# Differential attention with routed experts on one Trainium2 core: q/k/v projections five token tiles ahead of the scores instead of four

## The chip, the cores and the metric

The kernel runs on one core of one Trainium2 chip. The metric is the device time of one execution in microseconds (us). The engines named below are TensorE (PE; its weight loads are shown apart as PEld), VectorE (DVE), ScalarE (ACT), GpSimd (POOL) and SyncE (SP), which only issues DMAs. Each engine takes its instructions in the order in which it was given them.

## The reference, cut to what matters

One layer: RMS norm, differential attention, residual, RMS norm, a mixture of experts, residual. 1024 tokens, 1024 channels, 8 heads, two 64-wide halves of q and k in each head, float32 throughout.

```python
q, k, v = jnp.split(x @ w_in, [2 * H * dh, 4 * H * dh], axis=-1)
q = rmsnorm(q.reshape(B, T, H, 2, dh), q_gain) * (dh ** -0.5)
k = rmsnorm(k.reshape(B, T, H, 2, dh), k_gain)
sc = jnp.einsum('bqhcd,bkhcd->bhcqk', q[:, s:e], k[:, :e])
sc = jnp.where(dist >= 0, sc - slopes * dist, -jnp.inf)
p = jax.nn.softmax(sc, axis=-1)
pd = p[:, :, 0] - lam * p[:, :, 1]
o = rmsnorm(einsum('bhqk,bkhe->bqhe', pd, v[:, :e]), subln) * (1 - lambda_init)
x = x + o.reshape(B, T, H * 2 * dh) @ w_out
x = x + hier_moe(rmsnorm(x, norm_ffn))   # 16 experts, two for each token
```

## The kernel before

The tokens are cut into 8 tiles of 128 and the work of the attention into 64 steps, one for each pair of head h and tile t, numbered g = 8h + t. One loop (L765) runs over g; what it calls in one turn is issued in that order to each engine, and no scheduler moves it (`tc.manual_schedule()`, L37). Turn g does for its own tile the scores (`scores`, two matmuls per key block, high and low part), the bias and the row maximum on DVE (`biased`), the exponentials on ACT (`expo`) and the difference of the two softmaxes on DVE (`combine`). For the tile before, g - 1, it transposes the probabilities on PE (`pd_transpose`) and multiplies them with v (`pv`). The cost of scores, softmax and transposes grows with t, since a tile sees only the keys up to itself.

The same turn projects a tile that lies LEAD tiles ahead, q = g + LEAD: `qkv`, 24 matmuls of 384 columns in two parts of 12, each with the weight split in a high and a low part. At its end ACT and DVE take q, k and v out of PSUM and leave the sums of squares (ssq, L326). After every second tile `qk_norm` normalises the pair on POOL: 14 small instructions for the inverse root, then two products into the tile qn (L340). At odd g, `qk_transpose` (called from `crossings`, L351 and L353) transposes the pair that holds tile g + 1 on PE; ACT and DVE make the high and low parts KM, AH and AL from it. qn has one buffer, qk and ssq have two, vHL and vb thirteen.

The weights of the next heads are loaded by SP (`load_w`, at t == 3) and split into a high and a low part in 8 chunks (`split_w`: ACT makes wH, L243, DVE makes wL, L244), spread over the turns: one chunk in most turns, two at t = 3, none at t = 4.

When a head is done, `o_norm` normalises its output on POOL: 17 small instructions and two products (L458 to L464). For heads 0 to 5 this is issued at the end of the turn t = 1 of the next head, for head 6 already at t = 0 of head 7; `o_transpose` (L472) puts the result through PE at t = 4, for head 6 in the middle of the turn t = 2. For head 7 each tile has its own `o_norm1` on POOL (L522 to L528, 18 instructions), issued at the end of the turn after its scores, and its own `o_transpose1` on PE (L534).

As soon as no projections are left, g >= E0 = 64 - LEAD, the turns take up the output projection of tile e = g - E0 (`out_proj`, 48 matmuls), the residual (`residual`: store, square on ACT, inverse root on POOL) and the routing of the tiles before (`route_x`, `logits`, `route_r`, `route_i`). Before: e = 0 at g = 60, and the loop ends after g = 64 with e = 4. `late(5)` and `late(6)` do the two tiles after that without any attention in them, and `last` does tile 7. In `late(5)` o_transpose1(6) stands behind a third of an output projection; o_transpose1(7) follows after `late(5)`. Then the memory of the attention is given free (`es_att.close()`), and `moe_round` issues the loads of the first five weight tiles of the experts (1 MB each, L986, and three more as buffers come free) on SP before `late(6)`, which is called from `first_index`. Their first use is `split_h(0)` on ACT (L994), in the middle of `last`.

At the end of `last`, the rows of the tokens have been written to DRAM (xn_dram), and POOL gathers them by expert (L1011, L1017); the expert products begin with the gathered rows.

Of the kernel before, what the change touches and what calls it, by code (L numbers as in the profile page):

```python
# [7 lines left out]
F32 = mybir.dt.float32  # L8
F32R = mybir.dt.float32r
BF = mybir.dt.bfloat16  # L10
# [23 lines left out]
def trunk_layer_kernel(ctx, tc, a, out):  # L34
# [200 lines left out]
    def split_w(h, c):  # L235

        j = c // 3
        if c % 3 == 0:
            W["H", h, j] = w_tile([128, 3, 384], F32R, "wH")
            W["L", h, j] = w_tile([128, 3, 384], F32R, "wL")  # L240
        wh, wl, r = W["H", h, j][:, c % 3], W["L", h, j][:, c % 3], W["r", h, j][:, c % 3]
        g = gm[:, c:c + 1]
        act.activation(wh, r, AF.Copy, scale=g)  # L243
        vec.scalar_tensor_tensor(wl, r, g, f(wh), op0=OP.mult, op1=OP.subtract)  # L244
# [49 lines left out]
            other = slice(64 * (1 - c), 64 * (2 - c))  # L294
            vec.tensor_scalar(al[other, c], ident[other, None, :].to_broadcast([64, 2, 128]), 0.0, None, op0=OP.mult)
    QK, SS = {}, {}
    LEAD = 4

    def qkv(h, t, part):
        if part == 0:  # L300
            if h == 0 and t < LEAD and t % 2:
                qkv.ps = psQ.tile([128, 384], F32, name="qkv", tag="po", bufs=1)
            elif (8 * h + t >= LEAD and (t - LEAD) % NT in (0, 2)):
                qkv.ps = psS.tile([128, 384], F32, name="qkv", tag="sc")
            else:
                qkv.ps = psQ.tile([128, 384], F32, name="qkv", tag="qkv", bufs=1)
        ps = qkv.ps
        for c in range(4 * part, 4 * part + 4):
            for x, w in ((0, "H"), (0, "L"), (1, "H")):
                pe.matmul(ps, lhsT=hT[t][:, x, c], rhs=W[w, h, c // 3][:, c % 3],  # L310
                          start=(c == 0 and x == 0 and w == "H"), stop=(c == 7 and x == 1))
        if part == 1:
            rs = RX[t]
            if t % 2 == 0:
                QK[h, t // 2] = att.tile([128, 2, 4, 64], F32, name="qk", bufs=2)
                SS[h, t // 2] = att.tile([128, 2, 4], F32, name="ssq", bufs=2)
            qk = QK[h, t // 2][:, t % 2]
            act.activation(qk.rearrange("p a b -> p (a b)"), ps[:, :256], AF.Copy, scale=rs)
            v = att.tile([128, 2, 128], F32R, name="vHL", bufs=13)
            vb = att.tile([128, 128], BF, name="vb", bufs=13)  # L320
            VV[h, t] = v, vb
            act.activation(v[:, 0], ps[:, 256:], AF.Copy, scale=rs)
            vec.scalar_tensor_tensor(v[:, 1], ps[:, 256:], rs, f(v[:, 0]), op0=OP.mult, op1=OP.subtract)  # L323
            sq = att.tile([128, 4, 64], F32, name="sqk")
            act.activation(sq.rearrange("p a b -> p (a b)"), qk.rearrange("p a b -> p (a b)"), AF.Square)
            vec.tensor_reduce(SS[h, t // 2][:, t % 2], sq, axis=AX.X, op=OP.add)  # L326
            act.activation(vb, f(v[:, 0]), AF.Copy)
# [173 lines left out]
    def load_o(t):  # L501
        ORAW[t] = att.tile([128, H - 2, 128], F32, name="oraw")
        sp.dma_start(ORAW[t], o_view[:, :H - 2, t * 128:(t + 1) * 128])
# [243 lines left out]

    E0, LATE = NT * H - LEAD, 5  # L750
    def more_tokens(q):
        if q + 2 < NT:
            transpose_x(q + 2)
# [10 lines left out]

    for g in range(-LEAD, E0 + LATE):  # L765
        h, t = divmod(g, NT)
        q = g + LEAD
        e = g - E0
        if t == 0 and 0 <= h < H:
            vec.tensor_scalar(bias, bias, 0.5, None, op0=OP.mult)  # L770
        on(scores, g)
        on(biased, g, 0)
        if g > 2:
            crossings(g, h, t)
        on(expo, g, 0)
        on(biased, g, 1)
        if e >= 0:
            on1(out_proj, e, 0)
        on(qkv, q, 0)
        if t == 2 and h == H - 1:  # L780
            o_transpose(h - 1)
        on(pd_transpose, g - 1)
        on(expo, g, 1)
        on(combine, g)
        if 0 <= h < H - 1:
            if h == 0:
                chunks = {0: (0, 1), 1: (2,), 2: (3, 4), 3: (5, 6, 7)}.get(t, ())
            else:
                chunks = {0: (3,), 1: (4,), 2: (5,), 3: (6, 7)}.get(t, ())
            for c in chunks:  # L790
                split_w(h + 1, c)
        if t >= 5 and 0 <= h < H - 2:
            split_w(h + 2, t - 5)
        if 0 < e + NT < NT - 1:
            c = e + NT - 1
            split_wout(c)
            if c + 4 < NK:
                load_wout(c + 4)
        if e == -1:
            prep_o(0)  # L800
        if e >= 0:
            on1(route_x, e - 1)
            on1(route_i, e - 3)
            on1(route_r, e - 2)
            on1(prep_o, e + 1)
            on1(load_o, e + 2)
            on1(load_res, e + 1)
            on1(out_proj, e, 1)
            on1(o_transpose1, e + 1)
            route(e - 1)  # L810
            on1(residual, e)
        if q == 0:
            transpose_x(1)
            norm_x((2, 3), pool)
        if g <= 2:
            crossings(g, h, t)
        on(qkv, q, 1)
        on(pv, g - 1)
        if q == 0:
            more_tokens(q)  # L820
        if q % 2 and q < NT * H:
            qk_norm(q // NT, q % NT // 2)
        if t == (1 if h < H - 1 else 0) and 0 < h < H:
            o_norm(h - 1)
        if q > 0:
            more_tokens(q)
        if g == -LEAD:
            load_params()
        if g == -LEAD + 1:
            lambda_and_gains()  # L830
            load_w(1)
        if e == -2:
            load_o(0)
        if g == 9:
            routing_constants()
        if t == 3 and 0 <= h < H - 2:
            load_w(h + 2)
        if g == E0 - NT - 1:
            load_gain()
            for c in range(4):  # L840
                load_wout(c)
        if e == -1:
            for c in (NK - 2, NK - 1):
                split_wout(c)
            o_transpose1(0)
            load_o(1)
            load_res(0)
        on1(o_norm1, g - 1 - NT * (H - 1))
    def late(e):

        out_proj(e, 0, 0, 4)
        route_x(e - 1)
        route_i(e - 3, None, "tp")
        route_r(e - 2)
        flush()
        if e == LATE:
            prep_o(e + 1)
            o_transpose1(e + 1)
            load_o(e + 2)
        if e + 1 < NT:  # L860
            load_res(e + 1)
        out_proj(e, 0, 4, NK)
        route(e - 1)
        out_proj(e, 1)
        residual(e)
# [77 lines left out]
        return other_experts  # L943

    late(LATE)
    prep_o(LATE + 2)
    o_transpose1(LATE + 2)
    es_att.close()


# [344 lines left out]
            start(part)  # L1295

    def first_index(start):
        for e in range(LATE + 1, NT - 1):
            late(e)
        return last(start)  # L1300

    moe_round(first_index)
# [26 lines left out]
```

## Time and profile before

| | |
|---|---|
| time, three runs | 1018.61, 1018.22, 1013.28 us; median 1018.22 |
| the profiled execution's own time | 1017.58 us |
| its span, first to last instruction | 1015.7 us |
| busy: PE, DVE, ACT, POOL | 941.3, 816.4, 746.0, 338.1 us |
| granted TensorE clock, mean | 0.983 of full speed |
| attention, output projection and routing | 0 to about 637 us |
| experts | about 637 to 1000 us |

The busy time of PE comes from modelled ends of pipelined matmuls, so it is read here by what is missing: the gaps in which PE waits, what ended them, and the stretch of the kernel in which they lie. A row of the timeline gives start, duration, engine, line, operation, output and inputs, and in brackets the idle time of the engine just before it and what ended it.

### The profile page before, as it was taken

What the parts mean: (1) busy time and instruction counts of PE and PEld (TensorE: products, weight loads), DVE (VectorE), ACT (ScalarE), POOL (GpSimd) and SP (SyncE); (2) the same over time, 40 slices, a digit from 0 to 9 for tenths busy, and PEclk for the clock granted to TensorE, in tenths of its full rate; (3) what the DMA queues carried; (4) which work ended last, traced back from release to release, by engine and by line L of the source; (5) the groups of instructions that cost most, each with busy time, mean ns of one, the idle gap of its engine ahead of it and who ended that gap; (6) DMA issues with size and microseconds to landing.
All of it is one profiled execution on the core that took longest, in us unless ns stands there. A gap on an engine that the chain in (4) does not pass through costs nothing. (4 is left out here: it accounts for less than half of the span.)

```text
span 1015.7 us, 20013 instructions
## 1 busy us (share of the span) xinstructions
PE 941.3 (93%) x7241; PEld 875.5 (86%) x7241; DVE 816.4 (80%) x1719; ACT 746.0 (73%) x1577; POOL 338.1 (33%) x1009
## 2 busy tenths in 40 slices
PE   8989999999999999998999998799999999999992
PEld 8889899998989999888788886689989999999982
DVE  5788787887888787887768769799888899889880
ACT  7777777777777777777643325489899989898971
POOL 4523624425252442517764622201122212122011
PEclk9999999999999999999999999899999999999997
DMA  6220200202011020311323376789999999999923
GB/s 213 84 66 1 64 22 1 84 2 84 1 50 35 2 84 1 125 44 57 111 87 110 127 291 248 263 298 321 344 340 339 341 352 332 339 324 337 339 55 52
DMA packets 75770, 161.72 MB, mean 159 GB/s; under 512 B 8712, under 2 KB 39440, under 8 KB 67472
## 3 DMA queue, kind: packets, MB, share of 16 engines
q1 hardware_dynamic: 70544, 141.87, 39.4%
q0 software_dynamic: 5120, 18.50, 7.9%
q8 instruction: 59, 0.97, 0.4%
q14 instruction: 47, 0.39, 0.1%
HBM read 139.05 MB, written 21.30 MB: 158 GB/s over the span
## 5 line engine op out<-in xcount | busy, mean ns | idle before, releaser
L310 PE MATMUL qkv<-wH,hT 128*128 128x384 f32 x1024 | 291.3, 346 | 8.1 <-DVE vHL L323 6.9
L1003 DVE TENSOR_TENSOR mL<-raw,mH 128x2048 bf16<-128x2048 f32 x95 | 215.7, 2284 | 5.7 <-ACT mH L994 5.6
L310 PEld LDWEIGHTS qkv<-wH,hT 128*128 128x128 f32 x1024 | 188.2, 189 | 12.1 <-DVE vHL L323 10.4
L994 ACT ACTIVATE mH<-raw 128x2048 fp32r<-128x2048 f32 x95 | 177.8, 1902 | 1.2 <-POOL rs_x L56 1.2
L310 PE MATMUL qkv<-wL,hT 128*128 128x384 f32 x512 | 172.2, 336 | 0.4 <-DVE wL L244 0.4
L1069 PE MATMUL gu<-xT,mH 128*128 128x280 f32 x1024 | 153.4, 299 | 2.4 <-DVE gt L1099 1.3
L1069 PEld LDWEIGHTS gu<-xT,mH 128*128 128x128 f32 x1024 | 136.4, 190 | 3.2 <-DVE gt L1099 1.8
L1203 POOL DMA_INDIRECT out_dram<-yo,sidx x20 | 33.7, 1687 | 282.3 <-ACT yo L1201 251.6
L404 ACT ACTIVATE st<-st,nm 128x256 f32<-128x256 f32 (+7 forms) x128 | 99.2, 775 | 15.8 <-DVE nm L400 14.5
L1074 PEld LDWEIGHTS <-mL 128*128 128x128 bf16 x1536 | 94.0, 97 | 6.2
L310 PEld LDWEIGHTS qkv<-wL,hT 128*128 128x128 f32 x512 | 97.1, 190 | 0.7 <-DVE wL L244 0.7
L400 DVE CUSTOM_DVE_ANT_0 st<-sc,bias 128x256 f32<-128x256 f32 (+7 forms) x128 | 93.6, 750 | 2.3 <-PE sc L392 0.2
L1069 PE MATMUL gu<-hx,mH 128*128 128x280 f32 x512 | 82.0, 302 | 6.8 <-DVE yT L1099 6.2
L449 ACT ACTIVATE sqo<-ou 128x128 f32<-128x128 f32 x64 | 19.9, 311 | 92.3 <-DVE ou L447 92.3
L425 DVE TENSOR_TENSOR pdL<-tp,pdH 128x512 bf16<-128x512 f32 (+2 forms) x96 | 50.6, 554 | 45.0 <-ACT pdH L424 45.0
L550 PE MATMUL op<-wo,oH 128*128 128x512 f32 x256 | 82.2, 403 | 0.3 <-DVE xres L553 0.3
L334 POOL TENSOR_SCALAR ssq<-ssq 128x8 f32<-128x8 f32 x32 | 6.3, 198 | 226.8 <-DVE ssq L326 226.6
L1069 PEld LDWEIGHTS gu<-hx,mH 128*128 128x128 f32 x512 | 68.8, 189 | 9.2 <-DVE yT L1099 8.2
L1074 PE MATMUL gu<-xb,mL 128*128 128x140 bf16 x1024 | 74.3, 224 | 0.0
L391 PE MATMUL sc<-KM,AH 128*128 128x384 f32 (+4 forms) x192 | 65.5, 347 | 0.0
L392 PE MATMUL sc<-KM,AL 128*128 128x384 f32 (+4 forms) x192 | 65.0, 344 | 0.0
L411 DVE SCALAR_TENSOR_TENSOR st<-st,sm,st 128x128 f32<-128x128 f32 (+3 forms) x64 | 62.8, 981 | 2.3
(238 smaller groups left out, 1996.8 us busy)
## 6 DMA issues: line engine op xcount, KB each, us to landing
raw<-in_moe_w_gate_dram SPq DMA_DIRECT2D x32, 1024.0 KB, 7.4
raw<-in_moe_w_up_dram SPq DMA_DIRECT2D x32, 1024.0 KB, 6.2
raw<-in_moe_w_down_dram SPq DMA_DIRECT2D x31, 1024.0 KB, 8.1
wraw<-in_da_w_in_dram SPq DMA_DIRECT2D x64, 192.0 KB, 3.1
out_dram<-xres SPq DMA_DIRECT2D x9, 512.0 KB
xraw<-in_x_dram SPq DMA_DIRECT2D x8, 512.0 KB, 5.5
woraw<-in_da_w_out_dram SPq DMA_DIRECT2D x8, 512.0 KB, 5.2
xres<-in_x_dram SPq DMA_DIRECT2D x8, 512.0 KB, 4.3
```

Source lines behind the costliest of these rows:

```text
L310: pe.matmul(ps, lhsT=hT[t][:, x, c], rhs=W[w, h, c // 3][:, c % 3], start=(c == 0 and x == 0 and w == "H"), stop=(c == 7 and x == 1))
L391: pe.matmul(ps[:, k, :wc], lhsT=AH[h, t][:, c], rhs=KM[h][:, c, ks], start=True, stop=False)
L392: pe.matmul(ps[:, k, :wc], lhsT=AL[h, t][:, c], rhs=KM[h][:, c, ks], start=False, stop=True)
L400: vec.tensor_tensor_reduce(sv, tiles[c][:, :n, :wc], bv, -1.0, 3e38, OP.add, OP.min, nm[:, c:c + 1])
L404: act.activation(st[c][:, :w], st[c][:, :w], AF.Exp, scale=-1.0, bias=nm[:, c:c + 1], accum_out=sm[:, c:c + 1])
L411: vec.scalar_tensor_tensor(st[0][:, :w], st[1][:, :w], sm[:, 3:4], st[0][:, :w], op0=OP.mult, op1=OP.add)
L425: vec.tensor_sub(pl[:, g:g + n], ps[:, :n], f(ph[:, g:g + n]))
L550: pe.matmul(ps, lhsT=o[:, c], rhs=wo[4 * half + c // 2][:, w, c % 2], start=(c == 0 and o is oh and w == 0), stop=(c == NK - 1 and o is ol))
L994: act.activation(WH[g], full[g], AF.Copy)
L1003: vec.tensor_sub(WL[g], full[g], f(WH[g]))
L1069: pe.matmul(res[i // 2][:, i % 2, :2 * CAP], lhsT=wh[:, c - c0, 128 * i:128 * i + 128], rhs=rhs[:, c].rearrange("p a b -> p (a b)"), start ...
L1074: pe.matmul(res[i // 2][:, i % 2, :CAP], lhsT=wl[:, c - c0, 128 * i:128 * i + 128], rhs=rb[:, c], start=False, stop=stop, skip_group_check ...
```

## The change

LEAD goes from 4 to 5, so q = g + 5: one tile more is projected before the first scores, and all that follows q moves by one turn against the scores. Loading the weights moves from t == 3 to t == 2, the chunks move one turn earlier (now two at t = 2, none at t = 3, one at t = 4). Since norms follow odd q, `qk_norm` is now issued at even g instead of odd g, three turns before its pair is transposed instead of two. The output projection starts at g = 59 and the loop still ends after g = 64, so it now reaches e = 5; `late(6)` alone follows it, holds `o_transpose1(7)` at the place where `late(5)` held o_transpose1(6), and stands ahead of `es_att.close()` and of the expert weight loads.

```diff
-    LEAD = 4
+    LEAD = 5
@@ qkv
-                QK[h, t // 2] = att.tile([128, 2, 4, 64], F32, name="qk", bufs=2)
-                SS[h, t // 2] = att.tile([128, 2, 4], F32, name="ssq", bufs=2)
+                QK[h, t // 2] = att.tile([128, 2, 4, 64], F32, name="qk", bufs=3)
+                SS[h, t // 2] = att.tile([128, 2, 4], F32, name="ssq", bufs=3)
-            v = att.tile([128, 2, 128], F32R, name="vHL", bufs=13)
-            vb = att.tile([128, 128], BF, name="vb", bufs=13)
+            v = att.tile([128, 2, 128], F32R, name="vHL", bufs=14)
+            vb = att.tile([128, 128], BF, name="vb", bufs=14)
@@ loop
-    E0, LATE = NT * H - LEAD, 5
+    E0, LATE = NT * H - LEAD, 6
-                chunks = {0: (0, 1), 1: (2,), 2: (3, 4), 3: (5, 6, 7)}.get(t, ())
+                chunks = {0: (0, 1, 2), 1: (3, 4), 2: (5, 6, 7)}.get(t, ())
-                chunks = {0: (3,), 1: (4,), 2: (5,), 3: (6, 7)}.get(t, ())
+                chunks = {0: (4,), 1: (5,), 2: (6, 7)}.get(t, ())
-        if t >= 5 and 0 <= h < H - 2:
-            split_w(h + 2, t - 5)
+        if t >= 4 and 0 <= h < H - 2:
+            split_w(h + 2, t - 4)
-        if t == 3 and 0 <= h < H - 2:
+        if t == 2 and 0 <= h < H - 2:
             load_w(h + 2)
@@ late
-        if e == LATE:
-            prep_o(e + 1)
-            o_transpose1(e + 1)
-            load_o(e + 2)
+        prep_o(e + 1)
+        o_transpose1(e + 1)
     late(LATE)
-    prep_o(LATE + 2)
-    o_transpose1(LATE + 2)
     es_att.close()
@@ first_index
-        for e in range(LATE + 1, NT - 1):
-            late(e)
         return last(start)
```

## Rows read from the trace of the kernel before

**Rows 1.** The busy time of each engine in four stretches of the kernel (us from the span's start): the start of the attention, its steady part, the end of that, and the turn to the output projection. Columns: stretch, its length, busy us and instructions of each engine, granted TensorE clock, share of the DMA engines, GB/s.

```profile
40.00:100.00 60.00, 54.01 (x346) 50.50 (x346) 49.36 (x118) 44.92 (x123) 16.88 (x72) 1.00 0.13 29
100.00:400.00 300.00, 287.19 (x1873) 269.70 (x1873) 244.22 (x590) 229.88 (x634) 118.12 (x435) 1.00 0.12 36
400.00:460.00 60.00, 56.58 (x365) 52.77 (x363) 48.94 (x114) 45.44 (x122) 21.66 (x78) 1.00 0.25 80
460.00:500.00 40.00, 34.95 (x193) 30.38 (x192) 31.19 (x65) 26.85 (x71) 31.10 (x97) 0.96 0.14 46
```

**Rows 2.** What PE waited for between 100 and 400 us, all of it: waiter, what ended the wait, us in total, times, longest.

```profile
PE tp L351 <- POOL qn L340: 4.9, 20, 0.3
PE qkv L310 <- DVE vHL L323: 4.4, 5, 1.1
PE tp L423 <- DVE AL L368: 3.5, 10, 0.4
```

**Rows 3.** The timeline of one pair's norm on POOL, from its first instruction to its last, and the transposes on PE that read it (head 3, turn t = 1).

```profile
216.40 0.20 POOL L334 TENSOR_SCALAR ssq<-ssq 128x8 f32<-128x8 f32 x1 [11.99 <-DVE ssq L326]
...
220.87 1.44 POOL L340 TENSOR_TENSOR qn<-qk,rs_qk 128x256 f32<-128x256 f32 x2
...
221.79 0.33 PE L351 MATMUL tp<-ident,qn 128*128 128x128 f32 x1 [0.18 <-POOL qn L340]
...
```

**Rows 4.** The same head at t = 3 and the start of t = 4: the low part of the probabilities on DVE and the product that needs it on PE, then the second of two weight chunks on DVE, and the first matmul of the next projection, which waits for vHL behind it.

```profile
239.14 0.56 DVE L425 TENSOR_TENSOR pdL<-tp,pdH 128x384 bf16<-128x384 f32 x1 [0.53 <-ACT pdH L424]
...
239.75 0.51 PE L436 MATMUL po<-vHL,pdH 128*128 128x256 f32 x2
...
242.03 1.14 DVE L244 SCALAR_TENSOR_TENSOR wL<-wraw,gm,wH 128x384 fp32r<-128x384 f32 x2
...
243.48 0.45 PE L310 MATMUL qkv<-wH,hT 128*128 128x384 f32 x1 [0.82 <-DVE vHL L323]
```

**Rows 5.** Busy time of the projection's matmuls alone (L310) between 100 and 400 us: length, PE busy and matmuls, PEld busy and loads, granted clock, DMA.

```profile
100.00:400.00 300.00, 185.98 (x960) 164.09 (x960) 1.00 0.12 36
```

**Rows 6.** The timeline of the last head from t = 0 to the first output projection, on DVE, POOL and PE: the sums of squares of the turn g = 56; the start of o_norm(6) and its last product; PE's waits for qn; o_transpose(6); the norm of one pair from first to last instruction; an o_norm1 from first to last; PE after its wait; POOL's part of the output weights; o_transpose1(1).

```profile
462.99 0.40 DVE L326 TENSOR_REDUCE ssq<-sqk 128x4 f32<-128x256 f32 x1
...
463.33 0.33 PE L351 MATMUL tp<-ident,qn 128*128 128x128 f32 x1 [1.28 <-POOL qn L340]
...
463.81 0.20 POOL L458 TENSOR_TENSOR epso<-sm 128x8 f32<-128x8 f32 x1
...
469.70 1.22 POOL L464 TENSOR_TENSOR ou<-ou,rs_o 128x512 f32<-128x512 f32 x1
...
471.59 1.04 PE L472 MATMUL tp<-ident,ou 128*128 128x128 f32 x8
...
472.68 0.20 POOL L334 TENSOR_SCALAR ssq<-ssq 128x8 f32<-128x8 f32 x1 [1.76 <-DVE ssq L326]
...
476.61 0.39 PE L391 MATMUL sc<-KM,AH 128*128 128x512 f32 x1
...
476.65 1.50 POOL L340 TENSOR_TENSOR qn<-qk,rs_qk 128x256 f32<-128x256 f32 x2
478.11 1.17 POOL L522 TENSOR_TENSOR eps<-sm 128x1 f32<-128x1 f32 x1
...
483.85 0.63 POOL L528 TENSOR_SCALAR ou<-ou,rs_o 128x128 f32<-128x128 f32 x1
...
485.11 0.50 PE L436 MATMUL po<-vHL,pdH 128*128 128x256 f32 x2 [1.85 <-DVE pdL L425]
...
497.02 2.38 POOL L499 TENSOR_TENSOR wo<-woraw,wo 128x1024 fp32r<-128x1024 f32 x1
...
500.73 0.27 PE L534 MATMUL tp<-ident,ou 128*128 128x128 f32 x1
```

**Rows 7.** The timeline at the end of the last head: POOL's inverse root for residual(4), o_norm1(7) from first to last instruction, and between them, on PE, o_transpose1(6) in `late(5)`.

```profile
573.89 0.19 POOL L575 TENSOR_SCALAR ss<-ss 128x1 f32<-128x1 f32 x1 [5.42 <-ACT xn L564]
...
578.01 0.39 PE L534 MATMUL tp<-ident,ou 128*128 128x128 f32 x1 [0.34 <-DVE rk L692]
...
579.21 0.21 POOL L522 TENSOR_TENSOR eps<-sm 128x1 f32<-128x1 f32 x1
...
585.13 0.65 POOL L528 TENSOR_SCALAR ou<-ou,rs_o 128x128 f32<-128x128 f32 x1
...
```

**Rows 8.** The granted clock just after PE's wait of 1.85 us, the DMA rate while the first expert weights are loaded, and that of the stretch behind it; columns as in rows 1.

```profile
487.00:489.00 2.00, 2.00 (x8) 1.80 (x8) 1.40 (x5) 0.79 (x5) 1.49 (x7) 0.50 0.19 57
...
...
600.00:620.00 20.00, 20.00 (x138) 17.06 (x137) 15.19 (x59) 6.34 (x12) 4.03 (x15) 1.00 1.02 400
...
620.00:631.00 11.00, 7.45 (x52) 4.56 (x52) 9.76 (x59) 9.66 (x11) 0.13 (x1) 0.92 0.42 164
```

**Rows 9.** The timeline of the first loads of expert weights and the store of residual(6) on SP, of the first split on ACT, and of the first gather on POOL; then, for the token rows written between 600 and 626 us, the time from issue to landing (minimum, median, maximum).

```profile
593.90 0.81 SPq L986 DMA_DIRECT2D raw<-in_moe_w_gate_dram  x2
...
605.28 0.34 SPq L570 DMA_DIRECT2D out_dram<-xres  x1
...
610.41 1.91 ACT L994 ACTIVATE mH<-raw 128x2048 fp32r<-128x2048 f32 x1 [1.16 <-POOL rs_x L56]
...
630.87 1.93 POOL L1011 DMA_INDIRECT xg<-xn_dram,gidx  x1 [11.78 <-DMA out_dram<-xres]
...
DMA to landing us min/median/max: 9.3/9.3/9.3
```

## The prediction

> **What bounds the kernel now.** I read the engine totals first: PE is busy for 941.3 of 1015.7 us, so a change that removes no matmul can win only gaps of PE. Then the stretches [rows 1]: in the steady part, 100 to 400 us, PE is idle 300 - 287.19 = 12.8 us, in 400 to 460 3.4, in 40 to 100 6.0, and in the 40 us around the turn to the output projection 5.0. DVE and ACT, busy 81% and 77% of the steady part, are not far behind PE. Third, the waits of PE in the steady part [rows 2]: 4.9 us end with qn from POOL, 4.4 with vHL from DVE, 3.5 with AL from DVE. A head takes 24 projection matmuls for each of 8 tiles; 960 matmuls are 5.02 heads of 59.8 us [rows 5], and per head the three are .98, .88 and .70 us, together 2.55.
>
> Why they exist is read from the timelines. The pair's norm begins at 216.40 and its last product ends at 222.3, beside the transposes that take it up piece by piece [rows 3]: just in time, a few tenths late. At t = 3 two weight chunks of 1.14 us each stand on DVE ahead of vHL, and the next projection waits .82 for it [rows 4]. Behind the attention, the last chains are those of POOL's norms, of the routing, and of the rows in DRAM that the gather reads [rows 6, 7, 9].
>
> **The change, part by part.** All times are on the clock of the profiled execution.
>
> *Steady heads.* The norm gets a whole turn more, so the qn waits go (-.98 a head). qn still has one buffer: the next pair's product must wait for the transposes of the last, but its sums and inverse root, 220.87 - 216.40 = 4.5 us [rows 3], are done ahead, so I put no new wait there. The two chunks stand at t = 2, where the next projection does not wait for the same PSUM buffer, so the vHL waits go too (-.88). Cover for them is DVE and ACT. At t = 3 DVE is done with pdL at 239.70 and PE takes it at 239.75 [rows 4]: PE cannot come earlier there, so the part of the qn gain made ahead of it, about .5 (an estimate, half of the qn waits of a head), comes back as a wait for pdL. The chunk at t = 4 may lengthen AL by a little. I take -1.3 a head; ends: -.5 (DVE and ACT give nearly all back) and -2.55 (every wait goes). Heads 1 to 7, up to 460 us, are 6.4 heads at the measured rate (100 to 460 is 6.0, and the last stretch before 100 some .4): -8.3 (-3.2 to -16.3).
>
> *First head.* Its transposes of the x tile ahead move to the lead-in, and its three chunks go to t = 0 and t = 2 instead of t = 3. Of 6.0 us idle [rows 1] I take -2.0, a third, as in the steady part about half goes and here chunks pile up; ends 0 and -4.
>
> *Turn to the output projection.* Now the norms of q and k follow even g, so at g = 56 qk_norm(7, 2) stands on POOL ahead of o_norm(6). POOL's queue decides: its sums come at 462.99 + .40 = 463.4; the norm takes 5.5 (472.68 to 478.15), o_norm(6) 7.1 (463.81 to 470.92), o_norm1(0) 6.4 (478.11 to 484.48) [rows 6], so these end at 468.9, 476.0 and 482.4. o_transpose(6) stands on PE at 471.59, or 470.1 without the wait of 1.28 for qn and its small follower: it waits some 5.9. Behind come the norm of the last pair (5.5, and some .6 for its sums), POOL's part of the output weights (2.38) and o_norm1(1) (6.4) [rows 6]: 497.3 for o_transpose1(1). By its own work PE would be there at about 496.3 (an estimate), after its second wait, of 2.3, at o_transpose1(0), so POOL's chain sets the end. The old o_transpose1(1) is at 500.73 [rows 6]. But the new kernel has then still to do the scores, transposes and product of tile 4 that the old one had behind it (2.7, an estimate: some ten matmuls of tile 4, taken at somewhat under the .39 of a score matmul and the .50 of a product [rows 6], since they overlap), and it started one projected tile later: 24 x 185.98/960 = 4.65 us [rows 5]. So 497.3 + 4.65 + 2.7 - 500.73 = +3.9; the old waits there, 1.85 for pdL among them, are in it. After that wait the granted clock is .50, the level of 1.2 GHz [rows 8]; a wait of 5.9 may do that too, so ends +2 and +6. Without POOL's queue in the way this would be about -1.
>
> *Turns g = 60 to 64.* Each holds a residual's inverse root and an o_norm1 on POOL, some 11 to 12 us for turns in which PE had little to wait before. +.4 (0 to +1.5).
>
> *Tail of the attention.* In the new late(6), o_transpose1(7) stands in the place of o_transpose1(6), at 578.01. What it needs, o_norm1(7), ends only at 585.78, as it begins at 579.21 behind the inverse root of residual(4) that began at 573.89 [rows 7]. No other work of PE stands between: +7.8. It falls to +6.5 if that root, 5.3 us, takes only the 4.0 that the pair's root took from 472.68 to 476.65 [rows 6], and is +9 if it is as much longer.
>
> *Expert weights.* es_att.close() and the loads now follow late(6) on SP: the first is issued after the store of residual(6), at 605.28 + .34, about 605.7, instead of 593.90 [rows 9]. Eight weight tiles of 1.049 MB are loaded early, with 1.6 MB of token rows between them: 10.0 MB at 400 GB/s [rows 8] is 24.9 us, to 630.6, and the rows of tile 7 in xn and out, 1.05 MB, make it 633.2. The gather was issued at 630.87, just after those rows had landed [rows 9]: +2.4. Of the queues that the step is moved past, SP's is this one; POOL's holds only the gather. Ends: 0, if the rows land as they do now (in 620 to 631 us the DMA ran at only 164 GB/s [rows 8]), and +9.3, if they need another 9.3 us as the ones written under weights did [rows 9]. Below nothing is excluded, as nothing gets earlier by it. The first split on ACT at 610.41 [rows 9] then comes some 2 us late, but the work of ACT behind it does not.
>
> The Trainium skill, page "DMA: Bandwidth & Descriptors", section "Queues, rings and completion order", speaks against this move: SP owns one queue row, descriptors of a row are taken in ring order on each DMA engine, and only between rows do the engines alternate, packet by packet. [...] No row of before shows the order within the queue.
>
> **The sum.** -8.3 - 2.0 + 3.9 + .4 + 7.8 + 2.4 = +4.2 us: 1017.58 + 4.2 = 1021.8. The median of the runs is .64 above the profiled execution; 1022.4.
>
> **Rivals.** *All waits of the attention go.* DVE and ACT follow, nothing comes back: -16.3 - 4 against losses of 14.5 is -5.8, 1012.4. It decides from 1.95 us a head, (14.5 - 2.0)/6.4, on: there the time is as before. For it: each wait that it removes has a plain cause. Against it: pdL ready .05 us ahead of its use [rows 4].
>
> *Half of the losses are covered.* The token rows land as now, and POOL's queue at the turn only takes the place of the old waits there (PE idle 5.0 of 40 us [rows 1]): without 2.4 and 3.9 it is -2.1, 1016.1. For it: the low DMA rate behind 620 us. Against it: 5.9 us is more than all that stood there.
>
> *The change does not do what it says.* The norm comes a turn earlier, but PE stays at the pace of DVE and ACT: -.5 a head and nothing in the first, -3.2 + 14.5 = +11.3, 1029.5. For it: shares of 81% and 77% in averages over short and long turns. Against it: the vHL wait is one of DVE's order, not of its amount.
>
> **How the numbers follow.** The forecast has .50, with a range of its own of 1018 to 1027; the first rival .15, the second .17, the third .18. The range goes from 1013, by the first rival, to 1030, past the third. Within .5% (about what a measurement of this kernel can tell from no change) is 1013.1 to 1023.3. Faster: .10 of the first rival and .02 of the second, .12. Slower: .23 of the forecast, which lies .9 below that bound, and the third, .41. Same: .27, .05 and .15, .47.
>
> **What would show it.** Right: PE's waits for qn at L351 and for vHL at L310 nearly gone from the steady part, with some new ones for pdL; PE waiting 5 to 6 us at L472 for POOL's ou and 1 to 3 at L534; PE waiting 7 to 8 us at L534 late, for L528; the loads of L986 behind the store of L570, and the gather some 2 us later against the end of the last routing. Wrong: steady turns as long as before (then the first term falls), qn still late (then one buffer binds), o_transpose(6) without a wait (then POOL's order was misread), or a last transpose that finds its norm done.

## The result and the profile after

Before 1015.81 us (median of 4 runs, 1013.28 to 1018.61), after 1028.88 us (4 runs, 1028.35 to 1034.72): ratio 1.013, 95% interval 1.0099 to 1.016: slower by 1.3%. In the comparisons below, with 9 to 29 runs of the kernel before each, its median was 1017.55 to 1018.51, so that the distance is 10 to 13 us. The profiled executions differ by 10.8 us (1017.58 and 1028.35), their spans by 10.9 (1015.7 and 1026.6), and it is these 10.9 that the following accounts for. The forecast was 1022.4.

Landmarks on PE that both kernels have, read from the trace: the first score of head 1, the first score of head 7, the matmul of the routing (L689) in `late(6)` and the next one in `last`, and the first expert product. In the kernel after, the last transpose of the attention stands between the two L689; in the kernel before it stands ahead of both. First the kernel before:

```profile
L391 PE MATMUL sc<-KM,AH x2: 223/248/274, 94.3 to 94.5; 128*128 128x128 f32 x2
...
L391 PE MATMUL sc<-KM,AH x1: 222/222/222, 454.3 to 454.3; 128*128 128x128 f32 x1
...
L689 PE MATMUL rk<-sel,before x2: 183/183/183, 594.2 to 608.6; 128*128 128x16 bf16 x2
...
L1069 PE MATMUL gu<-xT,mH x1: 602/602/602, 644.2 to 644.2; 128*128 128x280 f32 x1
```

and the kernel after:

```profile
L391 PE MATMUL sc<-KM,AH x1: 223/223/223, 101.0 to 101.0; 128*128 128x128 f32 x1
...
L391 PE MATMUL sc<-KM,AH x2: 223/248/274, 454.2 to 454.3; 128*128 128x128 f32 x2
...
L689 PE MATMUL rk<-sel,before x2: 183/183/183, 592.9 to 617.4; 128*128 128x16 bf16 x2
...
L1065 PE MATMUL gu<-xT,mH x2: 435/518/602, 655.4 to 655.8; 128*128 128x280 f32 x2
```

One projected tile, 4.65 us [rows 5], is done before the first scores instead of at the end, so a landmark inside the heads may lie 4.65 later without a loss. Against that:

| stretch | moved by | forecast | measured |
|---|---|---|---|
| up to head 1 | 94.3 to 101.0, less 4.65 | -2.0 | +2.1 |
| heads 1 to 6 | +6.7 to -.1 | -8.3 | -6.8 |
| head 7, turn, g = 60 to 64 | -.1 - 4.65 to -1.3 | +4.3 | +3.5 |
| wait for the last transpose | -1.3 to +8.8 | +7.8 | +10.1 |
| weights, rows, gather | +8.8 to +11.2 | +2.4 | +2.4 |
| sum, with -.3 behind it | | +4.2 | +10.9 |

The -8.3 of the forecast counts 6.4 heads; for the six heads between the landmarks it is -7.8. The rows are rounded to .1.

The first two stretches of [rows 1] in the kernel after, and all that PE waited for from 100 to 400 us, against [rows 2]:

```profile
40.00:100.00 60.00, 55.88 (x341) 52.51 (x342) 47.53 (x117) 45.72 (x124) 17.97 (x71) 0.97 0.13 29
100.00:400.00 300.00, 289.98 (x1916) 276.31 (x1915) 242.06 (x602) 232.53 (x647) 115.26 (x431) 1.00 0.12 36
```

```profile
PE po L436 <- DVE pdL L425: 7.5, 5, 1.7
PE tp L423 <- DVE AL L368: 2.4, 10, 0.3
```

The waits for qn and vHL are gone as forecast. A wait for pdL, which the steady part did not have, stands in their place, once a head: .83 us in head 1, 1.66 to 1.70 in heads 2 to 6. The timeline around it, head 3, end of t = 2 and t = 3, on ACT, DVE and PE:

```profile
235.80 1.92 DVE L244 SCALAR_TENSOR_TENSOR wL<-wraw,gm,wH 128x384 fp32r<-128x384 f32 x2
238.23 0.41 DVE L447 TENSOR_REDUCE ou<-po 128x128 f32<-128x256 f32 x1
238.67 0.31 ACT L449 ACTIVATE sqo<-ou 128x128 f32<-128x128 f32 x1 [1.74 <-DVE ou L447]
238.98 0.75 ACT L362 ACTIVATE KM<-tp 64x256 fp32r<-64x256 f32 x2
...
242.99 0.56 DVE L425 TENSOR_TENSOR pdL<-tp,pdH 128x384 bf16<-128x384 f32 x1 [0.52 <-ACT pdH L424]
...
243.60 0.50 PE L436 MATMUL po<-vHL,pdH 128*128 128x256 f32 x2 [1.67 <-DVE pdL L425]
```

Read it as a chain: ACT, though idle for 1.74 us, cannot begin KM, because the square of ou stands ahead of it in ACT's order, and ou stands on DVE behind the two chunks; PE's transposes that KM reads had begun by 237.05 us. Then KM, AH, the exponentials and pdH follow on ACT, and pdL is late. With four tiles ahead the two chunks stood at the end of t = 3, and t = 4 has no such crossing.

The turn to the output projection and the last transpose, on PE, POOL and SP, as in [rows 6, 7, 9]:

```profile
475.33 2.11 PE L472 MATMUL tp<-ident,ou 128*128 128x128 f32 x8 [4.24 <-POOL ou L464]
...
482.66 0.33 PE L534 MATMUL tp<-ident,ou 128*128 128x128 f32 x1 [1.79 <-POOL ou L528]
...
589.35 0.19 POOL L575 TENSOR_SCALAR ss<-ss 128x1 f32<-128x1 f32 x1 [5.54 <-ACT xn L564]
...
594.66 0.21 POOL L522 TENSOR_TENSOR eps<-sm 128x1 f32<-128x1 f32 x1
...
601.23 0.48 PE L534 MATMUL tp<-ident,ou 128*128 128x128 f32 x1 [8.11 <-POOL ou L528]
...
614.10 0.34 SPq L570 DMA_DIRECT2D out_dram<-xres  x1
614.61 1.87 SPq L982 DMA_DIRECT2D raw<-in_moe_w_gate_dram  x2
...
644.27 1.69 POOL L1007 DMA_INDIRECT xg<-xn_dram,gidx  x1 [16.36 <-DVE ia L188]
```

and the granted clock just behind the 8.11 us:

```profile
601.00:604.00 3.00, 2.77 (x7) 2.26 (x8) 0.35 (x1) 0.37 (x1) 0.18 (x1) 0.50 0.00 0
```

The waits named for these two places are there, the first shorter than named (4.24 us for 5 to 6), the last a little longer (8.11 for 7 to 8). The 10.1 of the tail are the wait and the matmuls at .50, the level of 1.2 GHz, behind it: up to 605 us, which cost some 2 us.

### The profile page after: what moved, and what is told of

The parts are those of the page before. It is cut to its first block, busy times and chain, and to the rows that moved or that the text cites. A ratio compares the mean times of both kernels' runs of the same rounds, so it can differ in the third digit from the quotient of the medians.

```text
span 1026.6 us, 20001 instructions
## 1 busy us (share of the span) xinstructions
PE 939.9 (92%) x7241; PEld 877.7 (85%) x7241; DVE 800.6 (78%) x1719; ACT 744.5 (73%) x1577; POOL 331.6 (32%) x1009
## 5 line engine op out<-in xcount | busy, mean ns | idle before, releaser
L310 PE MATMUL qkv<-wH,hT 128*128 128x384 f32 x1024 | 291.4, 347 | 1.7 <-ACT wH L243 1.2
L310 PEld LDWEIGHTS qkv<-wH,hT 128*128 128x128 f32 x1024 | 188.8, 189 | 4.1 <-DVE vHL L323 2.4
L310 PE MATMUL qkv<-wL,hT 128*128 128x384 f32 x512 | 172.5, 337 | 0.4 <-DVE wL L244 0.4
L310 PEld LDWEIGHTS qkv<-wL,hT 128*128 128x128 f32 x512 | 97.4, 190 | 0.8 <-DVE wL L244 0.7
L550 PEld LDWEIGHTS op<-wo,oH 128*128 128x128 f32 x256 | 47.9, 192 | 9.9 <-DVE xres L553 0.7
```

The costliest lines, as they stand in the source:

```text
L550: pe.matmul(ps, lhsT=o[:, c], rhs=wo[4 * half + c // 2][:, w, c % 2], start=(c == 0 and o is oh and w == 0), stop=(c == NK - 1 and o is ol))
```

## The experiments

Each ratio is to the kernel before, run beside the version. Where two versions are compared, their medians come from different comparisons, and the change itself has only four runs, 6 us apart from lowest to highest; a difference of 1 or 2 us between versions is therefore not shown by the times alone.

**The wait for pdL: where the chunks stand.** First an even spread, with five and with four tiles ahead:

```diff
-                chunks = {0: (4,), 1: (5,), 2: (6, 7)}.get(t, ())
+                chunks = {0: (5,), 1: (6,), 2: (7,)}.get(t, ())
-        if t >= 4 and 0 <= h < H - 2:
-            split_w(h + 2, t - 4)
+        if t >= 3 and 0 <= h < H - 2:
+            split_w(h + 2, t - 3)
```

> The changed kernel with one weight chunk in every turn (t = 3 to 7, then 0 to 2 of the next head) instead of two at t = 2 and none at t = 3. Theory (the two chunks on DVE and ACT at t = 2 make everything behind them late, and PE waits 1.67 us at t = 3 for pdL in each head): that wait falls under .5 us, the head from 58.7 to about 57.5 us, and the time by 6 to 8 us, to about 1021 to 1023. Rival (DVE and ACT are the bound of a head as a whole): the wait comes back at another turn, the head stays at 58.5 us or more, and the time moves by less than 2 us.

Measured 1042.72 us, ratio to before 1.0248 (1.0234 to 1.0262): 14 us worse than the change.

> The kernel before (four tiles ahead), with one weight chunk in every turn, t = 4 to 7 and then 0 to 3, instead of two at t = 3 and none at t = 4. Theory (where the chunks stand is worth as much as the fifth tile): PE's wait of about 1.05 us per head for vHL at t = 3 falls under .3, the head from 59.8 to about 59 us, and the time by 4 to 6 us against before; the waits for qn, about 1 us a head, stay. Rival (the chunk at t = 4 makes AL or pdL late by as much): no change within 2 us.

Measured 1039.20 us, ratio 1.0208 (1.0192 to 1.0224). Both theories missed, and both rivals, and the trace of the first says why:

```profile
236.20 0.62 DVE L244 SCALAR_TENSOR_TENSOR wL<-wraw,gm,wH 128x384 fp32r<-128x384 f32 x1 [1.55 <-PE qkv L310]
...
237.88 0.41 PE L423 MATMUL tp<-ident,st 128*128 128x128 f32 x2 [1.08 <-DVE ou L447]
...
240.58 1.36 DVE L411 SCALAR_TENSOR_TENSOR st<-st,sm,st 128x384 f32<-128x384 f32 x1
...
248.37 0.50 PE L436 MATMUL po<-vHL,pdH 128*128 128x256 f32 x2 [1.70 <-DVE pdL L425]
```

Chunk 6 has to wait for PE: its buffer is still read by the projection of this head's last tiles. So DVE stands still for 1.55 us with everything behind it; this is presumably why the last two chunks share a turn in both kernels. The wait of 1.70 did not fall, although one chunk was gone from ahead of it: the other work had moved under a POOL product, beside which the difference of the softmaxes on DVE took 1.36 us instead of .64. This run therefore does not price the double chunk.

The second pair leaves the chunks in their turns and moves only the low parts on DVE behind vHL, the sums of squares and ou:

```diff
         act.activation(wh, r, AF.Copy, scale=g)
-        vec.scalar_tensor_tensor(wl, r, g, f(wh), op0=OP.mult, op1=OP.subtract)
+        wait_w.append((wl, r, g, wh))
@@ loop
         on(pv, g - 1)
+        split_w_low()
```

> The changed kernel in which DVE makes the low parts of the weight chunks (wL) at the end of the turn, behind vHL, the sums of squares and the output ou of that turn, instead of ahead of them; ACT makes the high parts where it did. Theory (at t = 3 the chain is ou on DVE, its square on ACT, KM and AH on ACT, AL and the second row maximum on DVE, pdL; it starts late because two chunks of about .95 us stand ahead of ou at the end of t = 2): PE's wait for pdL at t = 3 falls from 1.67 to between 0 and .7 us, the head from 58.7 to about 57.5 us, the time by 5 to 9 us, to about 1020 to 1024. Rival (the chain is set by ACT and by PE itself, DVE only follows): the wait stays above 1.2 us and the time within 2 us.

Measured 1026.93 us, ratio 1.0086 (1.0066 to 1.0107), 2 us under the change.

> The kernel before (four tiles ahead), with the same edit: wL at the end of the turn, behind vHL, sums of squares and ou. Theory (the wait of about 1.05 us per head for vHL comes from the order on DVE alone, and needs no fifth tile to go): that wait goes, nothing else gets longer, and the time falls by 4 to 6 us against before. Rival (the low parts come too late for the next head's projection at t = 4, or pdL at t = 4 gets late): no gain, within 2 us or slower.

Measured 1014.05 us (12 runs), ratio .9957 (.9941 to .9973): faster than before by 4 us, as expected. All of PE's waits from 100 to 400 us, five tiles ahead and then four:

```profile
PE po L443 <- DVE pdL L432: 6.8, 5, 1.5
PE tp L430 <- DVE AL L375: 2.0, 10, 0.2
```

```profile
PE tp L358 <- POOL qn L347: 4.1, 16, 0.4
PE tp L430 <- DVE AL L375: 3.5, 10, 0.5
PE tp L430 <- DVE KM L373: 0.9, 4, 0.2
```

With four tiles the vHL wait of 4.4 is gone and nothing of its size came. With five, the wait for pdL only falls to 1.3 us a head, since the low parts now stand ahead of KM and AL of the crossing (they run from 238.38 to 240.25, KM begins at 240.89, pdL at 243.40). These are the rival's numbers, but not its reason: pdH on ACT was done at 242.79, and pdL follows on DVE without a gap behind the row maximum.

Then the crossing itself, one turn earlier for the pair concerned:

```diff
-        if g % 2 and 0 <= g + 1 < NT * H:
+        if g % 2 and t != 3 and 0 <= g + 1 < NT * H:
             qk_transpose((g + 1) // NT, (g + 1) % NT // 2)
+        if t == 2 and 0 <= h < H:
+            qk_transpose(h, 2)
```

> The changed kernel in which the third pair of each head (tiles 4 and 5) is transposed and split into KM, AH and AL at t = 2 instead of t = 3, which the norm three turns ahead allows. Theory (two weight chunks at the end of t = 2, straight ahead of a crossing at t = 3, make the chain to pdL too long for that one turn; with four tiles ahead they stood at the end of t = 3, ahead of a turn without a crossing): the wait of 1.67 us for pdL at t = 3 falls under .8, with no new wait above .8 at t = 2, and the time falls by 4 to 8 us. Rival (the work of ACT and DVE in t = 2 and t = 3 together is too much, wherever it stands): the wait moves to t = 2 and the time stays within 2 us or grows.

Measured 1027.69 us, ratio 1.0087 (1.0061 to 1.0114). Nearer to the rival: the wait moved to t = 2, where it is 1.17 us, and the time is 1 us under the change, within the noise. And the chunks, made heavier (chunk 7 twice at t = 2):

> The changed kernel with the last chunk of the weights split twice at t = 2 of each head but the first (three chunks' work instead of two, same result). Theory (the chunks at the end of t = 2 stand on the chain to pdL of the next turn): the wait at t = 3 grows from 1.67 by about the .95 us of one chunk, the time by 5 to 7 us. Rival (the chain is that of the crossing on ACT and DVE and starts with PE's transposes): the wait grows by less than .3 us and the time by less than 2 us.

Measured 1044.15 us, ratio 1.0254 (1.0226 to 1.0282), 15 us more than the change. The waits, and the granted clock in front of one of them (head 3), behind it, and later:

```profile
PE po L436 <- DVE pdL L425: 11.3, 5, 2.3
PE tp L423 <- DVE ou L447: 2.5, 4, 0.6
```

```profile
246.00:249.00 3.00, 0.76 (x5) 0.44 (x3) 2.26 (x6) 2.90 (x9) 2.38 (x8) 1.00 0.00 1
249.00:251.00 2.00, 1.98 (x9) 1.89 (x10) 1.82 (x6) 1.20 (x5) 0.00 (x0) 0.50 0.00 0
251.00:253.00 2.00, 2.00 (x13) 1.96 (x12) 1.45 (x4) 0.40 (x2) 0.00 (x0) 0.65 0.00 0
```

The wait grew from 1.67 to 2.25 to 2.28, a new one of .6 came at ou in five heads: the chunks are on the chain, by two thirds of their work. Over heads 1 to 6 of the profiled executions this kernel takes 14.9 us more, and the longer waits are 7.5 of them. Most of the rest is the clock: it was granted at .50 behind four of the six waits of 2.25 to 2.28 us (heads 2, 3, 4 and 6), and stayed at 1.00 behind the other two.

**The first head.** No chunks at its t = 1:

```diff
-                chunks = {0: (0, 1, 2), 1: (3, 4), 2: (5, 6, 7)}.get(t, ())
+                chunks = {0: (0, 1, 2, 3, 4), 2: (5, 6, 7)}.get(t, ())
```

> The changed kernel with five chunks at t = 0 of the first head and none at t = 1, instead of three and two. Theory (PE's wait of 2.0 us for AH at t = 2 of head 0 comes from two chunks, 1.11 us on ACT, ahead of KM and AH): that wait falls under 1 us, and of the 2 us that the first head lost about 1 comes back; the rest is the projected x tile in the lead-in. Rival (the five chunks at t = 0 push the same work on): the wait or its successors stay, no gain beyond .3 us in the first head.

Measured 1029.21 us, ratio 1.0108 (1.0077 to 1.0138), no gain in the median. PE's waits in that place, of 2.0 us in one piece in the changed kernel:

```profile
51.70 0.41 PE L351 MATMUL tp<-ident,qn 128*128 128x128 f32 x2 [0.97 <-DVE hT L279]
...
55.92 0.45 PE L391 MATMUL sc<-KM,AH 128*128 128x384 f32 x1 [1.00 <-ACT AH L369]
```

The rival: the same 2 us in two pieces, so x tiles and chunks only change places. The two pieces did not bring the clock down (1.00 from 56 to 58 us), as the one piece had (.50), and head 0 itself took 58.7 us from score to score, against 60.5; but six more kernels with the changed kernel's code there spread from 59.0 to 60.6.

**The turn to the output projection.** The last two norms of q and k one turn later, behind o_norm1:

```diff
-        if q % 2 and q < NT * H:
+        if q % 2 and q < NT * H - 4:
             qk_norm(q // NT, q % NT // 2)
...
         on1(o_norm1, g - 1 - NT * (H - 1))
+        if g in (NT * H - 7, NT * H - 5):
+            qk_norm(H - 1, 2 if g == NT * H - 7 else 3)
```

> The changed kernel with the last two norms of q and k of head 7 issued one turn later on POOL, each behind the o_norm1 of that turn, so that o_norm(6) and o_norm1(0) stand ahead of them. Theory (POOL's order makes o_transpose(6) wait 4.24 and o_transpose1(0) 1.79 us): the first wait goes, the second falls to under 1, and the time falls by 3 to 5 us, to about 1024 to 1026. Rival (POOL's whole queue sets the end, the order inside it only moves the wait): PE waits as long in all, at qn of the last pairs or at o_transpose1(1), and the time stays within 1.5 us.

Measured 1033.56 us, ratio 1.0164 (1.0147 to 1.018). The rival, and worse: the wait is as long and sits elsewhere. Of the profiled execution's 5.7 us against the change some 1.7 are a slower clock in an earlier head, which the last section shows.

```profile
480.42 0.33 PE L534 MATMUL tp<-ident,ou 128*128 128x128 f32 x1 [2.48 <-POOL ou L528]
...
486.13 1.04 PE L351 MATMUL tp<-ident,qn 128*128 128x128 f32 x2 [4.45 <-POOL qn L340]
```

Then o_norm(6) ahead of the norm, and o_norm1(0) on DVE:

```diff
     def o_norm1(t):
+        pool = vec if t == 0 else nc.gpsimd
...
-        r = rsqrt(e[:, 0:1], 1, att, "o1")
+        r = rsqrt(e[:, 0:1], 1, att, "o1", pool)
@@ loop
+        if t == 0 and h == H - 1:
+            o_norm(h - 1)
         if q % 2 and q < NT * H:
             qk_norm(q // NT, q % NT // 2)
-        if t == (1 if h < H - 1 else 0) and 0 < h < H:
+        if t == 1 and 0 < h < H - 1:
             o_norm(h - 1)
```

> The changed kernel with o_norm(6) ahead of the norm of q and k on POOL in turn g = 56, and o_norm1(0) on DVE instead of POOL. Theory (POOL's queue as a whole sets the turn to the output projection, so taking 6 us of work off it is what counts, not its order): the waits at o_transpose(6) and o_transpose1(0), 4.24 and 1.79 us, fall under 1 us together, with nothing above 1.5 us in their place, and the time falls by 4 to 7 us, to about 1022 to 1025. Rival (DVE is as full there, and pdL and oL come later by what POOL saves): less than 2 us.

Measured 1031.30 us (1026.28 to 1034.09), ratio 1.0128 (1.0099 to 1.0157). Again the rival: both waits for POOL are gone, and 3.66 us for pdL and 2.71 for oL, both DVE's, stand there.

```profile
480.40 0.58 PE L436 MATMUL po<-vHL,pdH 128*128 128x256 f32 x1 [3.66 <-DVE pdL L425]
...
486.60 0.69 PE L353 MATMUL tp<-ident,qn 128*128 128x128 f32 x2 [2.71 <-DVE oL L537]
```

**The tail.** First POOL's order, o_norm1(7) ahead of the inverse root of residual(5):

```diff
-            on1(residual, e)
+            if e < LATE - 1:
+                on1(residual, e)
...
         on1(o_norm1, g - 1 - NT * (H - 1))
+        if e == LATE - 1:
+            residual(e)
```

> The changed kernel with residual(5) issued at the end of the last turn, behind o_norm1(7) instead of ahead of it, so that POOL norms tile 7 before the inverse root of residual(5). Theory (o_transpose1(7) waits 8.11 us only because o_norm1(7) stands behind that root): the wait falls under 3 us and the half clock behind it shrinks or goes; the time falls by 6 to 9 us, to about 1020 to 1023. Rival (what hangs on residual(5), its square on ACT and the logits of tile 5, is as late and takes the place of the wait): less than 4 us gained.

Measured 1029.23 us, ratio 1.0129 (1.0106 to 1.0151), no gain. The wait only fell to 6.74 us, and neither theory had the reason: on DVE, ou of tile 7 stood behind the routing of the tiles before (in the kernel after, PE was done with its product at 587.5 us and ou began at 592.48), and POOL now waits for its square.

```profile
593.81 0.43 DVE L447 TENSOR_REDUCE ou<-po 128x128 f32<-128x256 f32 x1
...
594.81 0.21 POOL L524 TENSOR_SCALAR eps<-sso 128x1 f32<-128x1 f32 x1 [9.18 <-ACT sqo L449]
```

This kernel runs 1.35 us later there (its L689 in `late(6)` begins at 594.26 against 592.91). Counted from that matmul, the norm is held up until .55 us by DVE's order, where POOL's order held it up until 1.75: POOL's order was worth 1.4 of the 8.11 us, the rest is behind DVE's. Then PE's order:

```diff
-        prep_o(e + 1)
-        o_transpose1(e + 1)
...
-        out_proj(e, 1)
+        out_proj(e, 1, 0, 4)
+        prep_o(e + 1)
+        o_transpose1(e + 1)
+        out_proj(e, 1, 4, NK)
```

> The changed kernel with o_transpose1(7) and its preparation moved on PE from behind the first third of the output projection of tile 6 to behind three quarters of it. Theory (the last transpose is only asked for too early; nothing else hangs on it): the wait of 8.11 us falls under 1 us, the half clock behind it goes, and the time falls by 8 to 10 us, to about 1019 to 1021. Rival (the tail behind it, the weights and the rows in DRAM, sets the end): the wait moves to the gathered rows and less than 5 us is gained.

Measured 1020.75 us (12 runs), ratio 1.0031 (1.0013 to 1.0049): 8 us less than the change. The transpose at 603.23 has no wait ahead of it. Adding the earlier end of the attention's memory (es_att.close() and the loads directly behind that transpose, the rest of late(6) behind them):

> The changed kernel with o_transpose1(7) behind three quarters of the output projection of tile 6, and with es_att.close() and the weight loads right behind that transpose instead of behind the whole of late(6). Theory: the 8 us of the transpose as in the kernel with that edit alone, and of the 2.3 us of the weights 1 to 2 us more, since the loads start some 4 us earlier: about 1018.5 to 1020. Rival (the weights' place costs nothing): as with that edit alone, 1020.7.

Measured 1019.65 us, ratio 1.0016 (.9999 to 1.0032), 1.1 us better, the least that was expected; the two intervals overlap, so the gain is not clear of noise. And the weights alone, in the kernel before:

```diff
     o_transpose1(LATE + 2)
+    late(LATE + 1)
     es_att.close()
...
-        for e in range(LATE + 1, NT - 1):
-            late(e)
         return last(start)
```

> The kernel before with late(6) ahead of es_att.close() and of the loads of the expert weights, as the change has it, and nothing else changed. Theory (the token rows that the gather needs stand behind the weights, which are issued some 12 us later): PE's wait for the first gathered rows grows from 1 us (and 4.5 at the second) by 2 to 3 us, and the time by 2 to 3 us against before. Rival (the DMA engines have room enough behind 620 us): within 1 us of before.

Measured 1021.36 us, ratio 1.0022 (1.0008 to 1.0037): +2.85 us against the runs beside it. PE now waits 7.02 us for the first gathered rows (second row below) and not for the others; in the kernel before it waited 1.03 us for the first and 4.48 for the others (first row):

```profile
641.94 1.09 PE L1029 MATMUL tp<-ident,xgr 48*128 48x48 f32 x8 [4.48 <-DMA xgr<-xn_dram,gidx]
...
645.44 0.87 PE L1047 MATMUL tp<-ident,xg 128*128 128x128 f32 x3 [7.02 <-DMA xg<-xn_dram,gidx]
```

**What helps, together,** with five tiles ahead: the late low parts, the late transpose, the earlier loads.

> The changed kernel with the low parts of the chunks at the end of the turn, with the late transpose and with the earlier weight loads: every edit that helped with five tiles ahead. Theory (the gains add up, 2 + 8 + 1.5 us): 1016 to 1018, even with before, and slower than four tiles ahead with the order of the low parts alone (1014.05). Rival (with its waits gone the fifth tile gives more than four tiles can): under 1014.

Measured 1018.06 us, ratio .9994 (.9975 to 1.0014): even with before.

> The changed kernel with the low parts at the end of the turn, the third pair transposed at t = 2, the late transpose of tile 7 and the earlier weight loads. Theory (each gains by itself, and the crossing at t = 2 and the late low parts work on the same wait): 1015 to 1018, no better than four tiles ahead with the low parts late (1014.05). Rival (both together clear the wait, which neither does alone): 1010 to 1013.

Measured 1018.54 us, ratio 1.0003 (.9987 to 1.0019), just above the 1015 to 1018 of the theory. PE's waits for pdL in a steady head are down to .86 us at t = 2 and .23 later. No version with five tiles ahead came near the 1014.05 us of four tiles with the low parts late (defer_low_lead4), the fastest median here. Between the same landmarks, and with one projected tile allowed for, the profiled execution of all_lead5 (span 1017.2 us) differs from that one (1012.3) by -5.7 us in heads 1 to 6, +2.8 up to head 1, +4.4 from head 7 to the first L689, +1.0 between the two L689 and +2.4 up to the first expert product: the fifth tile still gains in the steady heads, and loses more in the start, the turn and the weights.

## Why the prediction came out as it did

The place of each gain and loss was right but for the first head, where a gain was put and none came, and the range held the time, near its upper end. The sum was 6.7 us too low, so that "no change" was given the better chance and a slower kernel was measured. Three terms failed: the first head (-2.0, measured +2.1, of which 2.0 are a draw of the execution), the tail (+7.8, measured +10.1, as the clock behind the wait was put at nothing) and the steady heads (-7.8 for six of them, measured -6.8, as the new wait for pdL was put at .5 and is 1.67). By its steps:

*Steady heads: sized nearly right, in part by luck.* -6.8 us for -7.8. The step that "about .5" of the qn gain comes back as a wait for pdL was mis-sized: it is 1.67 us. What made up for it is not in PE's waits: from 100 to 400 us they fell by 2.9 us, some .6 a head, while a head became 1.1 us shorter; the other half lies in time that the profile counts as busy, and no run shows where. I took pdL's lateness to follow from PE coming earlier alone, and put the doubled chunks at t = 2 at no cost, since the next projection has another PSUM buffer. But they also stand ahead of ou, and ou of the square on ACT, and that of the crossing of t = 3. Tripled chunks lengthened the wait by .6 and made another of .6; low parts behind ou, and the crossing at t = 2, each shortened or moved it. No run made it go, so that the two chunks are on its chain is shown, that they are all of its cause is not. That ACT and DVE bound the short turns of a head at all is the third rival's mechanism, with a smaller price.

*First head: no gain.* -2.0 was a share taken from the steady part; +2.1 was measured in the profiled executions. PE waited for the first x tile .66 us before (first row) and 2.65 after (second row; the third is the kernel after too):

```profile
12.57 1.09 PE L274 MATMUL tp<-ident,xraw 128*128 128x128 f32 x8 [0.66 <-DMA xraw<-in_x_dram]
...
12.96 1.09 PE L274 MATMUL tp<-ident,xraw 128*128 128x128 f32 x8 [2.65 <-DMA xraw<-in_x_dram]
...
54.03 0.44 PE L391 MATMUL sc<-KM,AH 128*128 128x384 f32 x1 [2.00 <-ACT AH L369]
```

In other kernels equal up to that point this wait lies between nothing and 2.8, so 2.0 us of the +2.1 are a draw of the execution. The landmark itself spreads as much: seven kernels with the changed kernel's code up to it have the first score of head 1 at 98.9 to 101.0 us, two with that of the kernel before at 94.3 and 96.1. Less 4.65 us this is -1.9 to +2.1, or, with the wait for the x tile taken off each, +.1 to +1.8: a gain of 2.0 is not there, the sign of the 2.1 is not shown. As to why, the idle times ahead of a later x tile (1.27 and .43 us before) are 1.97 and .53 after (for the longer the profile names nothing that ended it), and the new 2.00 for AH replaces 1.2 for vHL and .7 for hT; the clock was .50 behind it (56 to 58 us). The text has the three chunks of t = 3 go to t = 0 and t = 2, but the diff puts one more at t = 1 too; without chunks at t = 1 (head0_chunks) that wait was 1.00.

*Turn to the output projection: right within 1 us.* +3.5 with the turns behind it, for +4.3. o_transpose(6) waited 4.24 for 5.9, o_transpose1(0) 1.79 for 2.3, and a wait of 1.18 for oL on DVE was not in the sum. What the runs add is that the orders tried on POOL are not the lever, and that DVE has no room there for o_norm1(0): with it on DVE, DVE's waits stand where POOL's were. DVE relieved was not tried.

*Tail: place and cause of the wait right, price short.* 8.11 us of wait for 7.8; I left out the clock behind it (.50 for 3 us and more), though the text priced that at the turn. And the norm's place behind the inverse root on POOL was the smaller of two causes, 1.4 us; without it DVE's order, which the text did not look at, still left 6.74. What helped was to ask for the transpose later.

*Expert weights: the total right, in part by luck.* +2.4 for +2.4, and +2.85 measured alone. But the gather came later than the sum has it: it was issued at 630.87 and 644.27 us, the last L689 at 626.82 and 635.64, so it moved by 4.6 us against the end of the routing and not by 2.4. PE lost only half of that, since the wait of 4.48 us for the rest of the gathered rows, which it had in the kernel before, is gone; the prediction does not name that wait, and why the rest came sooner after the first rows is open. What held the gather up is on SP: the last of the early weights, issued at 621.45 us, took 19 us to land, the rows of xn issued at 628.07, 634.05 and 636.67 landed at 641.9, 643.1 and 643.3, in the order of issue. The profile names DVE's ia for the gather's wait, but the gather begins .9 us after the last of these landings here, and .9 after it in before_late_weights and tail_and_weights too. The Trainium skill's "DMA: Bandwidth & Descriptors" has in "Queues, rings and completion order" that a row's descriptors are taken in ring order on each DMA engine, and that completion need not follow it; the order of landing here agrees with the first, and no run here shows the second.

Of the rivals, none came out as a whole. The first failed at the point that it named, DVE and ACT. The second's cover for the losses did not exist. In the third the losses were larger than in its sum and the gain better; that its 1029.5 lies next to the measured time is chance.

## What to carry to other kernels

One more stage of lead removes the waits that it is aimed at, but the whole schedule turns by one step against work that does not turn with it (here crossings at odd turns and buffers that come free at one point of the head), so lay each engine's order of one steady period side by side, old and new, and look for what now stands ahead of a chain's first link. Before adding lead, try the order on the engine that ends the wait: here moving the low parts of the chunks behind vHL took its wait away with four tiles ahead, and 4 us of the time. At the end of a pipeline price each wait of TensorE together with the granted clock behind it, as the trace shows it.

## What the runs showed that I had not expected

The clock behind a wait near 1.7 us was not the same from execution to execution. In the changed kernel, and in turn_norm_later, which has the same instructions up to there, PE waited in the same place of the same head. First the kernel after, where the clock stayed at 1.00, then the other, where it fell to .53, the level of 1.2 GHz for most of the stretch:

```profile
361.06 0.50 PE L436 MATMUL po<-vHL,pdH 128*128 128x256 f32 x2 [1.67 <-DVE pdL L425]
...
361.00:363.00 2.00, 1.94 (x15) 1.89 (x16) 1.79 (x7) 1.25 (x6) 0.29 (x1) 1.00 0.00 0
```

```profile
361.08 0.50 PE L436 MATMUL po<-vHL,pdH 128*128 128x256 f32 x2 [1.68 <-DVE pdL L425]
...
362.00:364.00 2.00, 2.00 (x12) 1.96 (x11) 2.00 (x7) 0.67 (x4) 0.00 (x0) 0.62 0.00 0
364.00:366.00 2.00, 2.00 (x10) 2.00 (x9) 0.78 (x4) 1.42 (x3) 0.00 (x0) 0.53 0.00 0
```

That cost 1.6 us there: the head took 60.4 us from score to score instead of 58.7. In the profiled executions of these two and of five more kernels with the same steady heads, there are 34 waits of 1.66 to 1.73 us, and five of them, in different heads, were followed by such a fall (a mean of .63 to .69 over the next 4 us), the others by 1.00. With such a wait in each of five heads, the runs of one kernel can spread: the four of the change reach from 1028.35 to 1034.72 us at a mean clock of .976 to .969. That the clock is what sets this spread was not tried by itself.
